# Gate projections moved into seven-product column pairs, with the two plain products of every pair made into filler units of their own

## The chip, the cores and the metric

The kernel runs on one core of one Trainium2 chip. The metric is the device time of one execution in microseconds, as the median of several runs. Engines are named as in the profile: PE is TensorE (matmuls), PEld its weight loads, DVE is VectorE, ACT is ScalarE, POOL is GpSimd, and SP is the engine whose queue issues the DMAs.

## What is computed

A decoder trunk of two layers on 1024 tokens of width 1024. Cut to what matters here:

```python
h = rmsnorm(x, norm1[l])
proj = h @ w_in[l]                        # 1024 x 5120
qa, ka, va, qb, kb, vb, gate_pre = split(proj)
o_a = dilated_mixture(qa, ka, va)         # 12 heads: 4 near, 8 far (two groups)
o_b = stick_breaking_attention(qb, kb, vb)  # 4 heads
g_a, g_b = halves of sigmoid(gate_pre + b_gate[l])
merged = g_a * (o_a @ w_br[l, :256]) + g_b * (o_b @ w_br[l, 256:])
x = x + merged @ w_o[l]
x = x + (gelu(conv(h2 @ w_up gate half)) * (h2 @ w_up value half)) @ w_down[l]
```

The change touches only `h @ w_in[l]`: the columns of the far heads' q, k and v, and the 2048 gate columns.

## The kernel before

**Numbers in two parts.** Every fp32 factor is split into a high and a low part (`split`, L123: ACT copies to the high part, DVE subtracts for the low part). One block product is then three matmuls: high x high, high x low, low x high. A matmul is 128 x 128 weights against 512 tokens.

**Units of projection work.** The normed activations `h` stand in SBUF as `H[n]`, n being the half of the tokens, with eight blocks of 128 features. `gate` (L1077) is a plain unit: it loads 128 gate columns (`weights`, L128), and for each token half runs `product` (L145) over eight blocks, 24 matmuls, copies the result out on ACT and stores it to the DRAM scratch `gs`. `pair` (L943) takes two groups of 128 columns at a time and computes their four results (two column groups, two token halves) with seven block products in place of eight, as Strassen's scheme in Winograd's form does, from sums of weight blocks (formed on POOL and DVE in the unit) and sums of activation blocks (`S[1]` to `S[4]`, formed once per layer in `block_sums`, L888). Each product is `seven` (L879), 12 matmuls. The products go in the order Q1, Q5, Q6, Q3, Q7, Q2, Q4. Two PSUM banks `pa` and `pc` are accumulated further after they have been read: Q1, Q6, Q7 and Q4 go into `pa`, Q5 and Q3 into `pc`, and Q2 has a bank of its own:

```python
yield from seven(pa, w7, S[3], False, True)
dve.tensor_tensor(view(u5), view(u5), grid(pa), ALU.add)
...
pb = bank("ps", "i_b")
yield from seven(pb, w2, half(1, 1), True, True)
...
for word in seven(pa, w4, S[4], False, True):
```

Of the 16 gate column groups per layer, eight are done by `gate` (`PLAIN`, L42) and eight by four `pair_gate` (L1066). Far keys and queries are four `pair_kq` (L1016), far values two `pair_v` (L1039), whose results are also transposed on PE (`v_t`, L1045). So a layer has ten pairs.

**What sets the order.** PE's order is written by the program: `manual_schedule` for PE. ACT, DVE, POOL and SP are ordered by a scheduler. In the attention part of a layer, `attend` (L306) walks the items of attention: stage B (16 stick-breaking items), N (4 near items), T (16 far items). After each of their steps it calls `Dense.advance` (L279) with a rate, and that many steps of filler go in between. One filler step is six matmuls, up to a `yield`. `Dense.choose` (L203) takes first the units in `main` whose conditions hold, then the `plain` ones, then the `seven` ones. A `seven` unit of `main` waits until `plain` is empty. The next unit is made ready while the present one runs: one step for a plain unit, six steps (`READY`, L36), given out at each "turn", for a pair. `RATE` (L41) holds the rates of B, N and the two halves of T. The far items need all far values and the keys of their half, so between N and T some pairs run alone: the pure filler phase. `finish` (L299) drains what is left after the last far item. Then follow the branches with the gates (`br_ps`), `wo_chunk` and the FFN, which the change leaves alone.

**Buffers.** PSUM tags "ps", "s", "t", "o" have two banks each. SBUF tag "pt" (L114) has six buffers of 128 x 512, used by attention and projections, "wr" two for raw weights and for the pair's `u`, "wh" and "wl" four each for split weights, "ql" two for the pairs' raw weights `in_a`.

## Time and profile before

| | |
|---|---|
| median of 3 runs | 2729.11 us (2728.45 to 2729.51) |
| span of the profiled execution | 2728.5 us |
| PE busy | 2677.8 us |
| DVE, ACT, POOL busy | 2016.5, 1353.4, 672.3 us |
| DMA engines busy, over the span | 46.2% |

A row of the stretches view reads: stretch in us, its length, then the busy time of PE, PEld, DVE, ACT and POOL with the number of instructions in brackets, the granted PE clock as a share of full speed, the busy share of the DMA engines, and GB/s. A row of the waits reads: the engine, what waited and its line, behind what; then us in total, how often, and the longest. A row of the timeline reads: start in us, duration, engine, line, operation, and in brackets the idle time before it with what ended it. A row by groups ends with busy us, mean ns of one, and the idle time before. A DMA row ends with the KB of one and the us to its landing. Matmuls are pipelined: a row's duration is longer than the distance to the next start. Attention of layer 0 lies at about 80 to 585 us, that of layer 1 at about 1400 to 1940 us.

### The profile page before, as it was taken

What the parts mean: (1) busy time and instruction counts of PE and PEld (TensorE: products, weight loads), DVE (VectorE), ACT (ScalarE), POOL (GpSimd) and SP (SyncE); (2) the same over time, 40 slices, a digit from 0 to 9 for tenths busy, and PEclk for the clock granted to TensorE, in tenths of its full rate; (3) what the DMA queues carried; (4) which work ended last, traced back from release to release, by engine and by line L of the source; (5) the groups of instructions that cost most, each with busy time, mean ns of one, the idle gap of its engine ahead of it and who ended that gap; (6) DMA issues with size and microseconds to landing.
All of it is one profiled execution on the core that took longest, in us unless ns stands there. A gap on an engine that the chain in (4) does not pass through costs nothing.

```text
span 2728.5 us, 36794 instructions
## 1 busy us (share of the span) xinstructions
PE 2677.8 (98%) x13194; PEld 2245.8 (82%) x13194; DVE 2016.5 (74%) x2976; ACT 1353.4 (50%) x2494; POOL 672.3 (25%) x485
## 2 busy tenths in 40 slices
PE   8999999989999999999999999999999999999999
PEld 8878888878888888888888788888788888888888
DVE  5877656665689888897658776565858888998865
ACT  5655545455455555532346565454635455554225
POOL 1005111112224343421120051211212343443210
PEclk9999999999999999999999999999999999999999
DMA  5012268554334444598410122784732444446863
GB/s 152 21 50 82 63 173 256 183 196 142 93 120 143 155 143 159 188 336 313 175 47 27 52 78 73 198 257 165 250 97 74 147 150 151 170 140 244 331 251 123
DMA packets 356738, 420.52 MB, mean 154 GB/s; under 512 B 20700, under 2 KB 285260, under 8 KB 355020
## 3 DMA queue, kind: packets, MB, share of 16 engines
q1 hardware_dynamic: 356556, 418.18, 46.2%
q8 instruction: 104, 1.70, 0.3%
q14 instruction: 78, 0.64, 0.1%
HBM read 278.59 MB, written 139.53 MB: 153 GB/s over the span
## 4 chain that ended last, share of the span: by engine, by line
PE 66%; DVE 8%; issue 2%; ACT 1%; DMA 1%; POOL 0%; DVEq 0%; ACTq 0%; SPq 0%; POOLq 0%
PE u_a L882 5%; PE u_a L883 5%; PE u_a L884 5%; PE d_ps L1584 4%; PE d_ps L1586 4%; PE d_ps L1585 4%; PE u_c L883 3%; PE u_c L882 3%; PE u_c L884 3%; PE o_ps L150 2%; PE o_ps L151 2%; PE o_ps L152 2%; PE i_a L882 1%; PE u_b L884 1%; PE u_b L882 1%
## 5 line engine op out<-in xcount | busy, mean ns | idle before, releaser
L125 DVE TENSOR_TENSOR w_lo<-up_a,w_hi 128x512 fp32r<-128x512 f32 x240 | 237.4, 996 | 20.5 <-ACT w_hi L124 20.5
L124 ACT CAST w_hi<-up_a 128x512 fp32r<-128x512 f32 x240 | 149.4, 622 | 183.8 <-PE u_a L883 45.4
L1592 DVE TENSOR_TENSOR x<-x,d_ps 128x512 f32<-128x512 f32 (+1 forms) x228 | 151.9, 671 | 77.4 <-PE d_ps L1586 76.1
L1323 POOL TENSOR_TENSOR cv<-cv 128x512 f32<-128x512 f32 x88 | 132.3, 1516 | 249.4 <-DVE cv L1318 139.6
L125 DVE TENSOR_TENSOR w_lo<-w_raw,w_hi 128x512 fp32r<-128x512 f32 x152 | 113.5, 751 | 67.0 <-ACT w_hi L124 63.6
L125 DVE TENSOR_TENSOR g<-cv,g 128x512 fp32r<-128x512 f32 x154 | 152.5, 991 | 5.2 <-ACT g L124 2.7
L124 ACT CAST w_hi<-w_raw 128x512 fp32r<-128x512 f32 x152 | 94.1, 620 | 124.9 <-PE o_ps L151 66.2
L125 DVE TENSOR_TENSOR w_lo<-in_a,w_hi 128x512 fp32r<-128x512 f32 x120 | 87.9, 732 | 82.4 <-ACT w_hi L124 82.1
L124 ACT CAST w_hi<-in_a 128x512 fp32r<-128x512 f32 x120 | 74.5, 621 | 132.3 <-PE i_c L883 52.0
L1584 PE MATMUL d_ps<-gd_in,w_hi 128*128 128x512 f32 (+1 forms) x340 | 130.5, 384 | 1.6 <-issue 0.7
L1586 PE MATMUL d_ps<-gd_in,w_lo 128*128 128x512 f32 (+1 forms) x340 | 129.8, 382 | 0.0
L1585 PE MATMUL d_ps<-gd_in,w_hi 128*128 128x512 f32 (+1 forms) x340 | 129.8, 382 | 0.0
L882 PE MATMUL u_a<-hh,w_hi 128*128 128x512 f32 x320 | 124.6, 390 | 0.7 <-DVE u L1474 0.7
L883 PE MATMUL u_a<-t_lo,w_hi 128*128 128x512 f32 x320 | 124.5, 389 | 0.0
L884 PE MATMUL u_a<-t_hi,w_lo 128*128 128x512 f32 x320 | 124.5, 389 | 0.0
L882 PE MATMUL u_a<-t_hi,w_hi 128*128 128x512 f32 x320 | 124.5, 389 | 0.0
L883 PE MATMUL u_a<-hl,w_hi 128*128 128x512 f32 x320 | 124.5, 389 | 0.0
L884 PE MATMUL u_a<-hh,w_lo 128*128 128x512 f32 x320 | 124.5, 389 | 0.0
L622 DVE TENSOR_TENSOR_SCAN stay<-stay,zero 128x128 f32<-128x128 f32 (+3 forms) x64 | 86.8, 1357 | 38.7 <-ACT stay L620 38.6
L1584 PE MATMUL d_ps<-gd_in,wd 128*128 128x512 f32 (+1 forms) x292 | 113.9, 390 | 0.0
L124 ACT CAST g<-cv 128x512 fp32r<-128x512 f32 x154 | 94.9, 616 | 37.1 <-POOL cv L1323 29.7
L1586 PE MATMUL d_ps<-gd_in,wd 128*128 128x512 f32 (+1 forms) x292 | 112.8, 386 | 0.0
(398 smaller groups left out, 8655.8 us busy)
## 6 DMA issues: line engine op xcount, KB each, us to landing
gd<-g SPq DMA_DIRECT2D x154, 512.0 KB, 3.4
gd_in<-gd SPq DMA_DIRECT2D x154, 512.0 KB, 6.3
up_a<-in_w_up_dram SPq DMA_DIRECT2D x80, 512.0 KB, 5.6
t_kq<-tk SPq DMA_DIRECT2D x32, 768.0 KB, 5.3
wd_raw<-in_w_down_dram SPq DMA_DIRECT2D x22, 1024.0 KB, 8.2
w_raw<-in_w_in_dram SPq DMA_DIRECT2D x80, 256.0 KB, 3.2
in_a<-in_w_in_dram SPq DMA_DIRECT2D x40, 512.0 KB, 4.9
gin<-gs SPq DMA_DIRECT2D x32, 512.0 KB, 4.1
```

What stands on the lines that cost most here:

```text
L124: act.copy(hi, src)
L125: dve.tensor_tensor(lo, src, f32(hi), ALU.subtract)
L150: pe.matmul(o, lh, rh, start=(first and i == 0), stop=False, skip_group_check=share)
L622: dve.tensor_tensor_scan(rev, rev, zero[:, 0:1].to_broadcast([P, L]), 1.0, ALU.mult, ALU.add)
L882: pe.matmul(o, w[0][:, c], rh, start=(first and i == 0), stop=False, skip_group_check=True)
L883: pe.matmul(o, w[0][:, c], rl, start=False, stop=False, skip_group_check=True)
L884: pe.matmul(o, w[1][:, c], rh, start=False, stop=(last and i == 3), skip_group_check=True)
L1323: return lambda: pool.tensor_tensor(dst, a, b, ALU.subtract)
L1584: pe.matmul(o[:, sub], wh[:, c], gh[:, sub], start=(i == 0 and k in (0, 4, 5)), stop=False, skip_group_check=True)
L1585: pe.matmul(o[:, sub], wh[:, c], gl[:, sub], start=False, stop=False, skip_group_check=True)
L1586: pe.matmul(o[:, sub], wl[:, c], gh[:, sub], start=False, stop=(i == m - 1), skip_group_check=True)
L1592: dve.tensor_tensor(x, x, o[:, sub], ALU.add)
```

## The change

All sixteen gate column groups of a layer become eight pairs; `gate` and `PLAIN` go. So a layer has 14 pairs. Each pair is cut in two generators. `ahead` is a plain unit: it computes Q1 = a11 x b11 (12 matmuls), copies it out on ACT and stores it in a DRAM scratch tile of the pair, then adds Q2 = a12 x b21 into the same bank (12 matmuls), which is the finished result for column group 0 and token half 1. `pair_rest` is the remaining seven unit, with five products in the order Q5, Q6, Q3, Q7, Q4; it loads Q1 back from DRAM into `u1` and adds it to the three other results. The plain list holds the `ahead` units of the four key/query pairs, the two value pairs and the eight gate pairs. The sum in place of `H[0]` (`S[4]`) now also waits for the units "01" and "v0". The two rates of stage T go from 0.72 and 0.62 to 0.88 and 0.77. The transposed values go through two small "pt" tiles instead of one of tag "p4".

```diff
-RATE = (0.68, 0.85, 0.72, 0.62)
-PLAIN = 8
+RATE = (0.68, 0.85, 0.88, 0.77)
...
-        series({"plain"}, 4, lambda i: further(4, b21, i), 1, 1)
+        series({"plain", "01", "v0"}, 4, lambda i: further(4, b21, i), 1, 1)
...
+        def ahead():
+
+            w = weights(w_in[l][:, offs[0] : offs[0] + P], P)
+            yield
+            o = bank("ps", "r_ps")
+            yield from product(o, [(w[k], h_part(1, k)) for k in range(4)], share=True)
+            t = small("q1s")
+            act.copy(view(t), grid(o))
+            nc.sync.dma_start(kept_product(key), t)
+            yield
+            yield from product(o, [(w[k], h_part(1, k)) for k in range(4, KD)], first=False, share=True)
+            put(0, 1, grid(o), True)
+            yield
+
+        return ahead, lambda: pair_rest(dense, l, offs, put, view, grid, kept_product(key))
+
+    def pair_rest(dense, l, offs, put, view, grid, kept):
...
         u1, u2 = u[:, HF:T], u[:, 0:HF]
+        nc.sync.dma_start(u1, kept)
...
-        w1 = piece(a11)
-        yield
...
         u5 = small("u5")
         pa, pc = bank("ps", "i_a"), bank("ps", "i_c")
-        yield from seven(pa, w1, half(1, 0), True, True)
-        act.copy(view(u1), grid(pa))
+        yield from seven(pc, w5, S[1], True, True)
+        dve.tensor_tensor(view(u5), view(u1), grid(pc), ALU.add)
         w7 = piece(u2)
-        yield
-        yield from seven(pc, w5, S[1], True, True)
-        act.copy(view(u5), grid(pc))
-        w2 = piece(a12)
-        yield
-        yield from seven(pa, w6, S[2], False, True)
-        act.copy(view(u2), grid(pa))
+        yield "turn"
+        yield
+        yield from seven(pa, w6, S[2], True, True)
+        dve.tensor_tensor(view(u2), view(u1), grid(pa), ALU.add)
...
-        pb = bank("ps", "i_b")
-        yield from seven(pb, w2, half(1, 1), True, True)
-        dve.tensor_tensor(view(u1), view(u1), grid(pb), ALU.add)
-        put(0, 1, u1, False)
-        yield "turn"
-        yield
         for word in seven(pa, w4, S[4], False, True):
             yield "turn"
             yield
-        put(1, 1, grid(pa), True)
+        dve.tensor_tensor(view(u1), view(u1), grid(pa), ALU.add)
+        put(1, 1, u1, False)
...
-            vv = sb.tile([P, 4, 2, P], F32R, tag="p4", bufs=4, name="vv")
+            for r in (0, 2):
...
+                vv = small("vv", F32R).rearrange("p (r h c) -> p r h c", r=2, h=2)
...
-        dense.plain = [gate(l, c) for c in range(PLAIN)]
-        dense.seven = [pair_gate(dense, l, e) for e in range(PLAIN // 2, KD)]
+        vs = {g: pair_v(dense, l, g) for g in (1, 2)}
+        kqs = {(g, pr): pair_kq(dense, l, g, pr) for pr in range(2) for g in (1, 2)}
+        gates = [pair_gate(dense, l, e) for e in range(KD)]
+        dense.plain = [a() for a, _ in [*kqs.values(), *vs.values(), *gates]]
+        dense.seven = [rest() for _, rest in gates]
```

More of the change, by code (lines that the diff above doesn't have):

```diff
@@ L109, in trunk_kernel, with kept_product @@
     dn = [dr.tile([4, T], F32, name=f"dn{i}") for i in range(2)]
+    first_half_product = {}
+    def kept_product(key):
+        if key not in first_half_product:
+            first_half_product[key] = dr.tile([P, HF], F32, name="q1")
+        return first_half_product[key]
     def bank(tag, name):
@@ L943, in pair @@
     def pair(dense, l, offs, tiled, put):
+        key = offs[0]
         def view(x, n=None):
@@ L1045, in turn @@
                 pe.transpose(tp[:, r * P : (r + 1) * P], f[:, r * P : (r + 1) * P], ident)
-            tw = tp.rearrange("p (r h c) -> p r h c", r=4, h=2)
-            vv = sb.tile([P, 4, 2, P], F32R, tag="p4", bufs=4, name="vv")
-            act.copy(vv[:, :, :, 0:64], tw)
-            dve.tensor_tensor(vv[:, :, :, 64:128], tw, f32(vv[:, :, :, 0:64]), ALU.subtract)
-            for h in range(2):
-                there = tv[c][h, :, :, g - 1, n * P : (n + 1) * P]
-                nc.sync.dma_start(there.rearrange("r p c -> p r c"), f32(vv[:, :, h, :]))
+            for r in (0, 2):
+                tw = tp[:, r * P : (r + 2) * P].rearrange("p (r h c) -> p r h c", r=2, h=2)
+                vv = small("vv", F32R).rearrange("p (r h c) -> p r h c", r=2, h=2)
+                act.copy(vv[:, :, :, 0:64], tw)
+                dve.tensor_tensor(vv[:, :, :, 64:128], tw, f32(vv[:, :, :, 0:64]), ALU.subtract)
+                for h in range(2):
+                    there = tv[c][h, r : r + 2, :, g - 1, n * P : (n + 1) * P]
+                    nc.sync.dma_start(there.rearrange("r p c -> p r c"), f32(vv[:, :, h, :]))
             if (c, n) == (1, 1):
@@ L1074, in pair_gate @@
         return pair(dense, l, (OFF_G + e * P, OFF_G + D + e * P), False, put)
-    def gate(l, c):
-        ab, e = c % 2, c // 2
-        cc = ab * KD + e
-        w = weights(w_in[l][:, OFF_G + cc * P : OFF_G + (cc + 1) * P], P)
-        yield
-        for n in range(2):
-            o = bank("ps", "g_ps")
-            yield from product(o, [(w[k], h_part(n, k)) for k in range(KD)])
-            t = small("gt")
-            act.copy(t, o)
-            nc.sync.dma_start(gs[e, n, :, ab, :], t)
-            yield
     def wo_chunk(l, n, e):
@@ L1139, in mixer @@
             *kq("0", 1, {"B17s"}, P, -SCALE),
-            (None, {"N11s"}, pair_v(dense, l, 1), True),
-            *((None, {"N11s"}, pair_kq(dense, l, g, 0), True) for g in (1, 2)),
-            (None, {"N11s"}, pair_v(dense, l, 2), True),
-            *((None, {"N11s"}, pair_kq(dense, l, g, 1), True) for g in (1, 2)),
+            (None, {"N11s"}, vs[1][1](), True),
+            *((None, {"N11s"}, kqs[g, 0][1](), True) for g in (1, 2)),
+            (None, {"N11s"}, vs[2][1](), True),
+            *((None, {"N11s"}, kqs[g, 1][1](), True) for g in (1, 2)),
         ]
```

## The prediction

> **What bounds the kernel now.** I read the page first, then busy time by stretches, then the waits of TensorE, then its timeline around the pairs.

> ```profile
> span 2728.5 us, 36794 instructions
> PE 2677.8 (98%) x13194; PEld 2245.8 (82%) x13194; DVE 2016.5 (74%) x2976; ACT 1353.4 (50%) x2494; POOL 672.3 (25%) x485
> PE 66%; DVE 8%; issue 2%; ACT 1%; DMA 1%; POOL 0%; DVEq 0%; ACTq 0%; SPq 0%; POOLq 0%
> ```
> ```profile
> 900.00:1000.00 100.00, 100.00 (x443) 82.84 (x442) 90.31 (x98) 52.73 (x84) 43.01 (x28) 1.00 0.44 151
> ```
> ```profile
> 340.00:380.00 40.00, 40.00 (x185) 32.86 (x184) 20.05 (x30) 16.84 (x29) 6.00 (x4) 1.00 0.56 153
> ```

> TensorE (PE) is busy 98% of the span and carries two thirds of the chain that ended last. So time follows what PE issues and where PE waits. In the FFN stretch 443 matmuls fill 100 us, 0.226 us each. The stretch 340 to 380 is the pure filler phase of layer 0: pairs alone, because the far items still lack their keys. DVE and ACT are only half busy there, so PE alone sets the pace. Idle PE is 50.7 us in all, and the named waits are mostly in attention:

> ```profile
> PE sb_t L633 <- DVE beta L623: 12.5, 10, 2.4
> PE o L808 <- DVE p1l L125: 5.6, 7, 1.6
> PE o L708 <- DVE p0l L125: 4.5, 2, 2.2
> ```

> **Term 1: fewer matmuls.** A gate column as `gate` costs 2 halves x 8 blocks x 3 = 48 matmuls, a pair of columns 96; with seven products a pair costs 7 x 4 x 3 = 84. Four gate pairs per layer change, so 4 x 12 x 2 layers = 96 matmuls go. The program's instruction counts agree: 13070 on PE before, 12974 after. The other ten pairs per layer keep their 84, now as 24 in `ahead` and 60 in `pair_rest`. What is one matmul worth? Starts of neighbours in the pure phase:

> ```profile
> 345.13 0.39 PE L883 MATMUL i_c<-hl,w_hi 128*128 128x512 f32 x1
> 345.36 0.39 PE L884 MATMUL i_c<-hh,w_lo 128*128 128x512 f32 x1
> 345.58 0.39 PE L882 MATMUL i_a<-t_hi,w_hi 128*128 128x512 f32 x1
> ```

> They start 0.225 us apart, though each is listed as 0.39. In the attention stages the step is about 0.23. So 96 x 0.23 = **-22 us**. [...]

> **Term 2: the sixth product no longer stands between the fifth and the seventh.** Before, `pair` runs Q7 into `pa`, then Q2 into its own bank, then Q4 into `pa`. DVE reads `pa` after Q7 while PE does the 12 matmuls of Q2. The change moves Q2 into `ahead`, so Q4 accumulates into `pa` directly behind Q7, and in the changed program Q4's first matmul waits for DVE's add of `pa` into `u5`. That is a new wait in all 28 pairs. Its length, from rows of the same hand-over:

> ```profile
> 345.85 0.69 DVE L994 TENSOR_TENSOR u<-u,i_c 128x512 f32<-128x512 f32 x1 [1.67 <-PE i_c L884]
> ```
> ```profile
> 595.00 0.68 DVE L1237 TENSOR_TENSOR gin<-gin,br_ps 128x512 f32<-128x512 f32 x1
> ```
> ```profile
> 595.73 0.50 PE L150 MATMUL br_ps<-oh_a,br_w 128*128 128x512 f32 x1 [0.56 <-DVE gin L1237]
> 596.07 0.39 PE L151 MATMUL br_ps<-ol_a,br_w 128*128 128x512 f32 x1
> ```

> An idle DVE starts 0.49 us after the last matmul started (345.36 to 345.85), works 0.69, and PE starts 0.05 after DVE ends (595.68 to 595.73). That is 1.23 instead of 0.23, so 1.00 lost; the first matmul after a wait then takes 0.34 until the next instead of 0.23, so 1.11 in all. What stands between Q7 and Q4 in the changed PE order shortens it: nothing in 16 of the 28 pairs, four small matmuls of a far item in 8 (0.41 us, 1921.58 to 1921.99 below), eight in 2, and eight with the sixteen of `join` in 2.

> ```profile
> 1921.58 0.28 PE L808 MATMUL o<-p1h,t_v 128*128 128x256 f32 x1
> 1921.99 0.44 PE L882 MATMUL i_c<-hh,w_hi 128*128 128x512 f32 x1
> ```

> 16 x 1.11 + 8 x 0.70 + 2 x 0.3 = **+24 us**. Behind the waiting Q4 stand all of PE's later work, the attention items too.

> **Term 3: the read in the middle of `ahead`.** Each of the 28 `ahead` units does 12 matmuls, has ACT copy the bank to `q1s`, then adds 12 more into the same bank. PE waits for that copy. The rows:

> ```profile
> 345.56 0.62 ACT L124 CAST w_hi<-in_a 128x512 fp32r<-128x512 f32 x1 [1.61 <-PE i_c L883]
> ```
> ```profile
> L1086 ACT COPY gt<-g_ps x32: 559/586/589, 144.5 to 1690.3; 128x512 f32<-128x512 f32 x32
> ```

> ACT starts 0.43 after the matmul (345.13 to 345.56) and copies a bank in 0.59. So 0.43 + 0.59 + 0.05 - 0.23 + 0.11 = 0.95, say 0.97. In 9 of the 14 units of a layer the ACT order has a weight split (0.62) right ahead of the copy, released by the last matmul but one; it pushes the copy back by some 0.29, making 1.26. Against that stands the attention work which the PE order has between the halves, from nothing to eight matmuls of scores. Priced by these rows (four score matmuls 0.47, four transposes 0.35), it sums to 6.9 us a layer:

> ```profile
> 300.20 0.28 PE L579 MATMUL z<-kt,qt 128*128 128x256 f32 x1
> 300.67 0.40 PE L150 MATMUL g_ps<-hh,w_hi 128*128 128x512 f32 x1
> ```
> ```profile
> 346.95 0.60 PE L1045 MATMUL v_t<-ident,u 128*128 128x128 f32 x4
> 347.30 0.48 PE L882 MATMUL i_a<-t_hi,w_hi 128*128 128x512 f32 x1
> ```

> (5 x 0.97 + 9 x 1.26 - 6.9) x 2 layers = **+19 us**.

> **What I cost at little or nothing.**

> ```profile
> q1 hardware_dynamic: 356556, 418.18, 46.2%
> ```
> ```profile
> w_raw<-in_w_in_dram SPq DMA_DIRECT2D x80, 256.0 KB, 3.2
> ```
> ```profile
> L125 DVE TENSOR_TENSOR w_lo<-w_raw,w_hi 128x512 fp32r<-128x512 f32 x152 | 113.5, 751 | 67.0 <-ACT w_hi L124 63.6
> ```

> The q1 store and reload (28 each, 256 KB): the reload is issued most of a pair before its use, the store long before that; without that cover each would cost a landing, 3.2 us by the row of that size. The reload waits on SP for a "wr" buffer, and behind it stand the next pair's `in_a` loads and the stores; that buffer's last reader is two pairs back, so I see no delay. `w_raw` gains 24 loads, `in_a` 16: with q1 some 29 MB on 418, and DMA is 46% busy. SP gains 128 issues; in the pure phase a key pair issues 16 stores instead of 20, now in 60 matmuls' time instead of 84. Splits: 24 more `w_hi` and `w_lo` pairs, 0.62 on ACT and 0.75 on DVE, all in stages B and N, where the attention chain itself runs over DVE; evictions that were ACT's become DVE's. The two `v_t` turns per layer that move into B take an "s" bank that scores use. The bound for all this is from below a gain: `RATE` puts more filler under each far item, so the 5.6 us of waits for `p1l` can go, and 72 matmuls instead of 30 are left behind the last `join` to cover the way into the branches, where the waits were

> ```profile
> PE x_t L1110 <- DMA xr<-in_x_dram: 3.2, 1, 3.2
> PE br_ps L150 <- DVE gin L1237: 2.7, 3, 1.7
> ```

> From above it is a longer DVE chain in B: 24 x 0.75 = 18 us of DVE, were it all on the chain. I take 0, nearest to the waits on either side, and keep -12 and +18 for the range.

> **Sum:** -22 + 24 + 19 = +21 on the profiled execution's 2728.5, so **2749 us**. Its span is 0.6 below the median of the three runs (2729.11), which is inside their spread (2728.45 to 2729.51); I add nothing for it.

> **Rivals.**
> *The waits are swallowed (faster).* Place: PE in the attention items. If the chain over DVE and ACT bounds B, N and T, a PE gap ahead of a wait for `beta`, `p0l` or `p1l` costs nothing. Then terms 3 and the far items' part of 2 vanish, the 16 bare gaps stay (17.8), and with the 5.9 us of waits into the branches gone: 2728.5 - 22 + 18 - 6 = 2719. For it: these waits exist. Against: they sum to 22.6 us, in 19 places, and must lie right behind the gaps. It is faster only when more than 26 us are swallowed or saved; between 15 and 26 it is no change.

> *The pair's preparation is late (slower still).* The seven products start with `w5`, which needs `a21 + a22`; `w1`, straight from the load, used to go first.

> ```profile
> in_a<-in_w_in_dram SPq DMA_DIRECT2D x40, 512.0 KB, 4.9
> ```
> ```profile
> L964 POOL TENSOR_TENSOR u<-in_a 128x512 f32<-128x512 f32 x20 | 29.1, 1455 | 119.0 <-DVE w_lo L125 61.7 <-DMA tk<-u 24.3 <-DMA tk<-kq_h 15.7
> ```

> From issue: 4.9 + 2 x 1.46 + 0.7 for `a11` on DVE = 8.5 us, and that DVE step stands ahead of the `u5` add in some pairs, which is due 48 matmuls = 10.9 us after the issue. 2.4 us are spare. Should loads land 4.2 us later with the pairs in quicker succession, 12 pairs lose some 1.8 each: 2749 + 22 = 2771.

> *The clock drops.* Stretches with waits show it:

> ```profile
> 580.00:620.00 40.00, 34.51 (x158) 27.56 (x158) 26.65 (x39) 23.58 (x41) 9.86 (x7) 0.96 0.65 222
> ```
> ```profile
> 1900.00:1940.00 40.00, 38.29 (x217) 32.68 (x216) 28.46 (x55) 25.38 (x51) 4.91 (x5) 1.00 0.63 220
> ```

> With 5.5 us idle the granted clock was 0.96 over 40 us, 1.6 us lost; with 1.7 us idle it stayed at 1.00. If each of the 16 bare gaps cost that: 2749 + 26 = 2775. The second row speaks against it. [...]

> That the change would not remove its 96 matmuls is no rival: the instruction order shows it.

> **Chances.** Forecast, 2735 to 2763: 0.62. Half swallowed, 2724 to 2734: 0.10. Swallowed, about 2719: 0.10. Late preparation, about 2771: 0.12. Clock, about 2775: 0.06. A range of **2724 to 2772** holds the first two and most of the late preparation, and takes in 2749 - 12 and 2749 + 18. A measurement of this kernel tells about 0.2% (5.5 us) from no change: faster 0.10 (the swallowed case), same 0.10 (half swallowed), slower 0.80.

> **What would show it.** The waits of PE should have a new row, `i_a` behind the DVE `u5` add, with 28 or fewer entries of 0.3 to 1.1 us and about 20 us in sum, and a new row `r_ps` behind ACT's `q1s` copy, about 19 us. PE's count falls by 96. The stretches of the pure phase should lose their 40.00 of 40.00. I am wrong if those rows are there but the `sb_t` and `o` rows fall by as much; if `i_c` or `u5` waits for POOL or a DMA show, the preparation is late; if the mean granted clock falls well below this row's, it is the clock.

> ```profile
> core 0: 2728.5 us, clock 0.997
> ```

## The result, and the profile after

The changed kernel takes 2799.82 us (median of 4 runs, 2797.74 to 2806.85) against 2729.19 us for the kernel before on the same chip (4 runs, 2728.45 to 2729.51). The ratio is 1.0261, 95% interval 1.0247 to 1.0276. It is slower, as forecast, but by 71 us where I had said 20. The profiled execution has a span of 2805.0 us, 76.5 more than before.

The page of the kernel after, the lines that answer to those shown of before; below them its mean granted clock, from the view by cores:

```profile
span 2805.0 us, 37073 instructions
PE 2691.6 (96%) x13098; PEld 2244.2 (80%) x13098; DVE 2070.0 (74%) x3104; ACT 1338.3 (48%) x2478; POOL 694.0 (25%) x509
PE 61%; DVE 8%; issue 3%; DMA 3%; ACT 2%; POOL 1%; SPq 0%; DVEq 0%; ACTq 0%; POOLq 0%
```
```profile
core 0: 2805.0 us, clock 0.988
```

PE has 96 matmuls less, and yet 13.8 us more busy time. Part of that comes with the waits: ahead of the gap shown further down (0.98 us, from 360.97 on) the last matmul counts with its listed 0.40 us, where neighbours start 0.23 apart, and the first behind it takes 0.33 until the next starts. So this gap adds some 0.27 us to the busy time. Another part is the clock, whose mean went from 0.997 to 0.988. Idle PE went from 50.7 to 113.4 us. Where it waits, in the waits of PE of the kernel after:

```profile
PE r_ps L155 <- ACT q1s L966: 26.1, 26, 3.0
PE i_a L887 <- DVE u L1019: 22.8, 24, 2.5
PE sb_t L638 <- DVE beta L628: 9.4, 8, 2.2
PE z L584 <- DVE st L795: 8.2, 5, 2.3
PE o L713 <- ACT p0h L129: 6.4, 2, 3.2
...
PE i_c L887 <- DVE u L1003: 3.9, 4, 2.1
PE z L584 <- ACT stay L625: 3.5, 3, 1.2
```

The first two rows are the hand-overs of terms 3 and 2. The other rows are waits of attention and of the pairs. `beta` is lower than it was (12.5), but `z` behind `st` had 1.4 us before and `o` behind `p0h` 0.5, and `i_c` behind a DVE add had no row at all. Busy time by stretches, the one that lost its 40.00 of 40.00, and the FFN stretch, which the change leaves as it was:

```profile
340.00:380.00 40.00, 36.26 (x169) 29.19 (x170) 26.33 (x46) 15.85 (x31) 5.99 (x5) 0.96 0.43 125
900.00:1000.00 100.00, 100.00 (x442) 82.81 (x442) 89.80 (x101) 51.41 (x81) 38.63 (x26) 1.00 0.48 164
```

All of the difference lies in the attention part of the two layers. The next table cuts it into stages by PE's timeline (a stage begins with the first matmul of its kind: `sb_t` for B, the first transpose of N, and so on; the pure filler phase ends with the first `z` from `t_kq`, T with the end of the last matmul of `join`). "Filler" counts the projection matmuls per layer in a stage. "Beyond its work" is the two layers' difference, less the change in filler at 0.23 us each.

| stage | filler before, after | us before (layers 0, 1) | us after | beyond its work |
|---|---|---|---|---|
| B | 558, 558 | 171.0, 170.0 | 178.8, 180.5 | +18 |
| N | 270, 270 | 87.7, 87.6 | 105.6, 105.0 | +35 |
| pure filler | 402, 258 | 95.3, 95.3 | 70.6, 72.3 | +18 |
| T | 420, 474 | 151.4, 149.8 | 177.7, 177.0 | +29 |
| rest, up to the first `br_ps` | 30, 72 | 6.7, 6.7 | 17.7, 17.8 | +3 |
| branches, up to the first `o_ps` | | 59.0, 46.0 | 51.8, 48.7 | -4 |

The sum is +99, and with the -22 of the 96 matmuls +77, the 76.5 of the two spans. B and N hold the same number of filler matmuls as before and are 53 us longer. The forecast had 19 us for them, all of it the waits for `q1s`; these waits lie in B and N and have 26 us of idle time.

How the two hand-overs look, in the timeline of the kernel after. Term 2, PE and then DVE:

```profile
360.57 0.40 PE L889 MATMUL i_a<-t_hi,w_lo 128*128 128x512 f32 x1
361.95 0.50 PE L887 MATMUL i_a<-hh,w_hi 128*128 128x512 f32 x1 [0.98 <-DVE u L1019]
362.28 0.40 PE L888 MATMUL i_a<-hl,w_hi 128*128 128x512 f32 x1
```
```profile
361.21 0.68 DVE L1019 TENSOR_TENSOR u<-u,i_a 128x512 f32<-128x512 f32 x1
```

Term 3, ACT and then PE:

```profile
285.44 0.62 ACT L129 CAST w_hi<-w_raw 128x512 fp32r<-128x512 f32 x1
286.08 0.59 ACT L966 COPY q1s<-r_ps 128x512 f32<-128x512 f32 x1
```
```profile
286.72 0.50 PE L155 MATMUL r_ps<-hh,w_hi 128*128 128x512 f32 x1 [1.10 <-ACT q1s L966]
287.06 0.40 PE L156 MATMUL r_ps<-hl,w_hi 128*128 128x512 f32 x1
287.29 0.56 PE L157 MATMUL r_ps<-hh,w_lo 128*128 128x512 f32 x1
287.65 0.63 PE L155 MATMUL r_ps<-hh,w_hi 128*128 128x512 f32 x1
```

The first, 0.98 us, is the gap that was priced. In the second, ACT does the split right ahead of the copy, as foreseen, and PE waits 1.10 us. But look at the last lines: at about 287.4 the matmuls turn slow. They are listed with 0.63 us instead of 0.40, and their starts lie 0.43 apart (287.65, and the next at 288.08) instead of 0.23. The stretches around that place, cut at 3.41 us:

```profile
284.00:287.41 3.41, 1.69 (x9) 1.08 (x8) 3.40 (x7) 2.57 (x5) 0.00 (x0) 0.99 0.28 77
287.41:290.82 3.41, 3.41 (x11) 2.66 (x10) 3.35 (x6) 0.48 (x1) 0.00 (x0) 0.51 0.44 147
290.82:294.24 3.42, 3.42 (x20) 2.93 (x19) 2.47 (x5) 1.92 (x4) 0.00 (x0) 1.00 0.24 84
```

The granted clock (the third number from the end) is 0.51 in the middle row: 11 matmuls in a full window where the next one has 20. In the row ahead of it PE is busy 1.69 of 3.41 us. That is half a window idle, and no single wait made it: 0.62 us for `p0l` at 285.00 and 1.10 us for `q1s`. So the gap of 1.10 us, with that of 0.62 us near it, cost another 1.7 us (half of the 3.41).

That is a pattern of the whole trace. The half-clock stretches last 3.4 us, in some cases 6.8, and within one run all begin on one grid of 3.41 us (after, the starts of the first and the last, 184.96 and 2024.75, lie 539 steps apart). In the kernel before there are four; the windows ahead of them hold 2.24 to 2.44 us of idle PE, and no other window of its two attention parts has more than 1.72. After, there are 15 (four of them double), behind windows with 1.67 to 3.11 us idle; five other windows with 1.73 to 1.78 were not followed by one. At half a stretch each (0.50 granted), and without the last microseconds of the span, half clock took up to 6.8 us before and up to 32.4 after: 25.6 of the 76.5. These times are upper ends, since PE also waits inside some of the stretches.

Where the 15 lie matters for the account below. The waits in the windows ahead of them are those for `q1s` (six windows, in two of them together with `p0l`, in one with `beta`), `beta`, `p0h`, `p1h`, `st` and `gin`. None lies behind a window in which `i_a` waits, and the two pure filler phases after have no half clock at all.

### The profile page after: what moved, and what is told of

It reads as the page before. It is cut to its first block, busy times and chain, and to the rows that moved or that the text cites. A ratio compares the mean times of both kernels' runs of the same rounds, so it can differ in the third digit from the quotient of the medians.

```text
span 2805.0 us, 37073 instructions
## 1 busy us (share of the span) xinstructions
PE 2691.6 (96%) x13098; PEld 2244.2 (80%) x13098; DVE 2070.0 (74%) x3104; ACT 1338.3 (48%) x2478; POOL 694.0 (25%) x509
## 4 chain that ended last, share of the span: by engine, by line
PE 61%; DVE 8%; issue 3%; DMA 3%; ACT 2%; POOL 1%; SPq 0%; DVEq 0%; ACTq 0%; POOLq 0%
PE u_a L887 5%; PE u_a L888 5%; PE u_a L889 5%; PE d_ps L1590 4%; PE d_ps L1591 4%; PE d_ps L1592 4%; PE u_c L888 3%; PE u_c L889 3%; PE u_c L887 3%; PE o_ps L155 2%; PE o_ps L157 2%; PE o_ps L156 2%; DVE w_lo L130 1%; PE u_b L889 1%; PE u_b L888 1%
## 5 line engine op out<-in xcount | busy, mean ns | idle before, releaser
L130 DVE TENSOR_TENSOR w_lo<-w_raw,w_hi 128x512 fp32r<-128x512 f32 x176 | 127.9, 730 | 80.7 <-ACT w_hi L129 80.2
L129 ACT CAST w_hi<-w_raw 128x512 fp32r<-128x512 f32 x176 | 109.1, 621 | 150.8 <-PE o_ps L156 70.4
L155 PE MATMUL r_ps<-hh,w_hi 128*128 128x512 f32 x224 | 98.6, 440 | 26.1 <-ACT q1s L966 26.1
L988 POOL TENSOR_TENSOR u<-in_a 128x512 f32<-128x512 f32 x28 | 36.8, 1314 | 336.2 <-DVE w_lo L130 89.2
## 6 DMA issues: line engine op xcount, KB each, us to landing
gd<-g SPq DMA_DIRECT2D x154, 512.0 KB, 3.6
gd_in<-gd SPq DMA_DIRECT2D x154, 512.0 KB, 6.7
up_a<-in_w_up_dram SPq DMA_DIRECT2D x80, 512.0 KB, 5.8
in_a<-in_w_in_dram SPq DMA_DIRECT2D x56, 512.0 KB, 5.5
w_raw<-in_w_in_dram SPq DMA_DIRECT2D x104, 256.0 KB, 3.0
gin<-gs SPq DMA_DIRECT2D x32, 512.0 KB, 4.5
```

Of the source, the lines that this page charges most:

```text
L129: act.copy(hi, src)
L130: dve.tensor_tensor(lo, src, f32(hi), ALU.subtract)
L155: pe.matmul(o, lh, rh, start=(first and i == 0), stop=False, skip_group_check=share)
```

## The experiments

Each was timed beside the kernel before on the same chip. That took 2732.18 us (7 runs) beside the first four, 2730.74 (7 runs) beside the second four, and 2731.09 (13 runs) beside the last four. Ratios are to these, with a 95% interval. Where two changed kernels from different sets are compared, the difference is given by the ratios (times 2731 us) and by the times.

Half clock is that of the one profiled execution of each kernel, without its first 30 us and its last microseconds, and it differs between executions of the same kernel. In the four executions of the kernel with both hand-overs mended, for example, the mean granted clock is 0.987 to 0.991, and 0.004 of its span is 11 us. In the ten executions of the kernel with gaps of one read it is 0.995 to 0.998. So differences of a few microseconds of half clock between two of these kernels are not shown to come from the edit.

### The five products in an order that alternates the two banks

The changed kernel with Q6, Q5, Q7, Q3, Q4, which alternate between `pa` and `pc`; the preparation follows that order.

```diff
-        w3 = piece(a11)
+        w7 = piece(u2)
...
+        yield from seven(pa, w6, S[2], True, True)
+        dve.tensor_tensor(view(u2), view(u1), grid(pa), ALU.add)
+        w3 = piece(a11)
...
         yield from seven(pc, w5, S[1], True, True)
         dve.tensor_tensor(view(u5), view(u1), grid(pc), ALU.add)
-        w7 = piece(u2)
...
-        yield from seven(pa, w6, S[2], True, True)
-        dve.tensor_tensor(view(u2), view(u1), grid(pa), ALU.add)
         w4 = piece(a22)
...
+        yield from seven(pa, w7, S[3], False, True)
...
         yield from seven(pc, w3, half(0, 1), False, True)
...
-        yield from seven(pa, w7, S[3], False, True)
```

> Only the order of the five products is changed: Q6, Q5, Q7, Q3, Q4, so that the banks alternate and twelve matmuls stand between a read of a bank and the next product into it. Theory gaps (the waits of PE between two runs of one bank cost their own length, and together with the other waits they pull the granted clock to half for whole stretches): the 22.8 us of waits for the u5 add go, with 3 us of slow restarts, and some 8 of the 18 half-clock stretches of the attention stages (each 1.7 us lost): 2800 - 26 - 13 = 2761, clock about 0.993. Rival load (the clock and the other new waits come from the added splits, stores and fetches): only the waits go, 2774, clock 0.989. Rival feed (the pairs are late in preparation anyway): the waits move to the weights, no more than 8 us gained.

Measured: 2779.29 us (2776.86 to 2781.99), ratio 1.0175 [1.016, 1.019]. The row `i_a` behind the `u5` add (22.8 us) is gone from the waits of PE. In its place `i_a` waits 4.4 us for the weight split of the product that now comes first, and `z` behind `st` has 11.4 us instead of 8.2. Half clock was 25.6 us instead of 32.4, but the mean clocks of the four executions (0.988 to 0.991) are those of the changed kernel (0.988 to 0.990).

What follows: the hand-over of term 2 was worth 20 us by the times and 23 by the ratios, about what its idle time of 22.8 says. Of the forecasts, the one that the waits alone would go (2774) came nearest; that the clock would come back with them (2761) is not borne out.

### Q1 and Q2 of `ahead` in two banks

The changed kernel, with Q2 in a bank of its own and DVE adding the two.

```diff
-            yield from product(o, [(w[k], h_part(1, k)) for k in range(4, KD)], first=False, share=True)
-            put(0, 1, grid(o), True)
+            o2 = bank("ps", "r2_ps")
+            yield from product(o2, [(w[k], h_part(1, k)) for k in range(4, KD)], share=True)
+            t2 = small("q2s")
+            dve.tensor_tensor(view(t2), view(t), grid(o2), ALU.add)
+            put(0, 1, t2, False)
```

> Only the unit ahead is changed: Q2 goes into a bank of its own, and DVE adds it to the copy of Q1, so PE need not wait for the copy. Theory gaps: the 26.1 us of waits for q1s go, with 3 us of restarts, and some 8 half-clock stretches: 2800 - 29 - 13 = 2758, clock about 0.993. Rival load: 2771, clock 0.989; and since the add moves from ACT to DVE in the stages B and N, where the chain runs over DVE, part of that would come back as waits for beta and p0l.

Measured: 2784.54 us (2779.3 to 2788.51), ratio 1.0193 [1.0172, 1.0213]; half clock 23.9 us in the profiled execution, which was the fastest of the four. N went from 105 to 96 us, B stayed at 179. In the waits of PE:

```profile
PE v_t L1063 <- DVE q2s L972: 4.8, 2, 2.4
PE r_ps L155 <- ACT q1s L966: 2.2, 2, 1.1
```

What follows: 24 of 26 us of the `q1s` wait went, and only 15 us of time (19 by the ratios) came back, less than either forecast. Part of the gaps was given back elsewhere: the transposes of the values now wait for the sum `q2s`. The four executions differ with the clock: 2779 and 2781 us at 0.991 and 0.990, 2788 and 2789 us at 0.987 and 0.988.

### Both together

The two diffs above in one kernel.

```diff
+        yield from seven(pc, w5, S[1], True, True)
+        dve.tensor_tensor(view(u5), view(u1), grid(pc), ALU.add)
...
+            o2 = bank("ps", "r2_ps")
```

> Both edits. Theory gaps: both rows of waits go, and the clock returns to about 0.996: 2800 - 55 - 22 = 2723, near the kernel before. Rival load: 2745, clock 0.989, with the new waits of z and o still there. If what the change saves on matmuls (22 us) were to show in full, 2710.

Measured: 2768.45 us (2765.69 to 2770.27), ratio 1.0134 [1.0119, 1.0149]; half clock 23.9 us in the profiled execution. So both hand-overs together are worth 31 us by the times, 35 by the ratios. Half clock is 8.5 us less than in the profiled execution of the changed kernel, but that one was the slowest of its four and this one the fastest of its four; the mean clock of the four executions is 0.9895 there and 0.9890 here. That the clock came back with the two waits is not shown. The kernel is still 36 us above before, with 2.2 us of my two waits left, and both forecasts (2723 and 2745) were far too low. The longest waits of PE now:

```profile
PE z L584 <- DVE st L795: 12.4, 6, 5.5
PE sb_t L638 <- DVE beta L628: 10.6, 10, 2.2
PE o L713 <- ACT p0h L129: 6.4, 2, 3.2
PE o L713 <- DVE p0l L130: 6.3, 8, 1.5
```

The wait for `st` had 8.2 us in the kernel after. In the waits of PE of the kernel before it was

```profile
PE z L579 <- DVE st L790: 1.4, 2, 0.7
```

Its longest case in layer 0 (4.93 us, soon after the start of T; the like place of layer 1 has 5.46) is read from the timelines of DVE and PE in this kernel:

```profile
436.99 0.69 DVE L994 TENSOR_TENSOR in_a<-in_a 128x512 f32<-128x512 f32 x1 [1.18 <-POOL in_a L992]
437.60 0.68 DVE L1030 TENSOR_TENSOR u<-u,i_a 128x512 f32<-128x512 f32 x1
438.19 1.29 DVE L130 TENSOR_TENSOR w_lo<-in_a,w_hi 128x512 fp32r<-128x512 f32 x2
439.40 0.68 DVE L130 TENSOR_TENSOR w_lo<-u,w_hi 128x512 fp32r<-128x512 f32 x1
440.00 1.75 DVE L1043 SCALAR_TENSOR_TENSOR u<-u,kq_h 128x512 fp32r<-128x512 f32 x1
441.67 0.41 DVE L795 CUSTOM_DVE_ANT_1 p<-z,bias 128x256 f32<-128x256 f32 x1
```
```profile
442.15 0.48 PE L584 MATMUL z<-t_kq 128*128 128x128 f32 x1 [4.93 <-DVE st L795]
```

DVE stood waiting 1.18 us, until 436.99, for POOL's sum of the next pair (`in_a`, the step called `a11` in the prediction), and its rows behind that start one after the other up to 441.67: an add of the pair, three splits, another step of the pair's results (L1043), and last the step of attention that PE needs. This is the rival of the late preparation, in a form that the prediction named: the DVE step of `a11` stands ahead of work that is due. In the waits of DVE of the kernel after, with no such row for `in_a` in before:

```profile
DVE in_a L991 <- POOL in_a L989: 37.2, 21, 3.6
```

### The old rates of T

The changed kernel with the old line.

```diff
-RATE = (0.68, 0.85, 0.88, 0.77)
+RATE = (0.68, 0.85, 0.72, 0.62)
```

> The changed kernel with the two rates of stage T put back to 0.72 and 0.62. Theory gaps: the pairs' waits stay the same in number, more of them after the last far item; less filler under each far item brings the waits for p1l back, some 3 us: 2800 to 2806. Rival load (the denser filler in T overloads DVE and the DMA queue there): 2785 to 2795.

Measured: 2797.68 us (2796.57 to 2803.28), ratio 1.0247 [1.0227, 1.0266], against 1.0261 [1.0247, 1.0276] of the change. T shrinks from 178 to 162 us in layer 0 and the rest behind it grows from 18 to 32.

What follows: the rates move filler from one place to another and neither cost nor gain anything that can be measured. The 29 us that T lost are not theirs.

### The sums of weights all on POOL

The kernel with both hand-overs mended, with the sum for `w5` first and the step of DVE moved to POOL, so that DVE's queue no longer waits there.

```diff
-        pool.tensor_tensor(u2, a11, a21, ALU.subtract)
-        pool.tensor_tensor(a21, a21, a22, ALU.add)
+        pool.tensor_tensor(u2, a21, a22, ALU.add)
+        pool.tensor_tensor(a21, a11, a21, ALU.subtract)
         yield
-        dve.tensor_tensor(a11, a21, a11, ALU.subtract)
-        w5 = piece(a21)
+        pool.tensor_tensor(a11, u2, a11, ALU.subtract)
+        w5 = piece(u2)
...
-        w7 = piece(u2)
+        w7 = piece(a21)
```

> The kernel with both edits, and in the pair's preparation the sum a21 + a22, which w5 waits for, is now formed first, and a11 on POOL in place of DVE. Theory late preparation (in the shorter pairs DVE stands in its queue before a11 until POOL and the loads are there, and the far items' reductions and the evictions stand behind it): the waits of DVE for POOL go, the waits of z for the reduction (12.4 us) fall below 6, the stages after N lose some 10 us a layer less: 2768 - 15 = 2753. Rival splits (what is left lies in B and N, from the added splits): 2765 to 2770. Rival DMA (the far items' fetches are late whatever the engines do): z still waits some 10 us, 2765.

Measured: 2755.4 us (2754.3 to 2758.71), ratio 1.0096 [1.0081, 1.0111]; half clock 18.8 us. The row of DVE behind POOL is gone, and PE's wait for `st` fell from 12.4 to 7.8 us (not below 6, as expected).

What follows: the late preparation was real and cost about 0.4%, some 10 us. The profiled execution has 5.1 us less half clock (23.9 to 18.8), but the mean clocks of the four executions overlap (0.987 to 0.991 without the edit, 0.989 to 0.993 with it), so how much of the 10 us came by way of the clock stays open.

### Half of the splits in `ahead`

The kernel with both hand-overs mended, but `ahead` loads and splits only the first four weight blocks and uses them for Q2 as well. The result of column group 0 and token half 1 is then not the reference's; the number of matmuls is the same.

```diff
...
-            w = weights(w_in[l][:, offs[0] : offs[0] + P], P)
+            w = 2 * weights(w_in[l][0:512, offs[0] : offs[0] + P], P, rows=4)
```

> The kernel with both edits, but each unit ahead loads and splits only the first four weight blocks and uses them for Q2 too: Q2 is computed from the wrong weights, and half of the units' splits and loads are left out. Theory splits (two splits of ACT and DVE for every 24 matmuls of filler in place of 48 lengthen B and N, whose PE work is the same as before): B falls from 179 to some 173 us and N from 96 to some 90, both layers: 2768 - 24 = 2744. Rival (the order of the units, v_t and the key stores in B make it): B and N stay within 2 us.

Measured: 2758.2 us (2754.43 to 2760.81), ratio 1.0103 [1.0088, 1.0118] against 1.0134 [1.0119, 1.0149] with all splits: 10 us less by the times, 8 by the ratios, for 28 splits and 28 loads less. N is 4 us shorter in each layer, B is unchanged (178 and 179).

### The kernel before, with more splits

The kernel before, its `gate` unit cut in one unit for each token half. So each half loads and splits its weights again: 16 more loads and splits per layer (32 in all; the change itself has 24 more in all), and twice as many units of half the size.

```diff
-    def gate(l, c):
+    def gate(l, c, n):
...
-        dense.plain = [gate(l, c) for c in range(PLAIN)]
+        dense.plain = [gate(l, c, n) for c in range(PLAIN) for n in range(2)]
```

> The kernel before with each plain gate unit cut in two, one for each token half, each loading and splitting its weights anew: 16 splits and loads more per layer, no new wait of PE on its own banks, nothing else. Theory splits: B and N grow by some 6 us each in each layer, with half-clock stretches: 2729 + 24 = 2753. Rival: the splits find room on ACT and DVE: 2729 to 2733.

Measured: 2744.61 us (2740.46 to 2748.0), ratio 1.0059 [1.0042, 1.0075]. N grew from 87.6 to 93.9 us in both layers, B did not (169.7 and 171.8). In the waits of PE of this kernel there is a row that the kernel after has too:

```profile
PE o L708 <- ACT p0h L124: 6.4, 2, 3.2
```

It is one wait of 3.2 us per layer, in N, and behind it lies a half-clock stretch of 6.8 us. `p0h` is the split of attention weights on ACT, the engine on which the weight splits (0.62 us each) are made. But ACT was not too busy. Its timeline, and DVE's, ahead of the wait at 257 us, and ACT at the same place of the kernel after:

```profile
252.35 0.62 ACT L124 CAST t_hi<-h_sum 128x512 fp32r<-128x512 f32 x1 [5.78 <-POOL h_sum L901]
253.40 0.42 DVE L595 TENSOR_TENSOR ob<-sb_o,fold 64x256 f32<-64x256 f32 x1 [5.26 <-ACT fold L594]
```
```profile
261.56 0.62 ACT L129 CAST t_hi<-h_sum 128x512 fp32r<-128x512 f32 x1 [5.78 <-POOL h_sum L906]
```

ACT stands idle for 5.78 us until POOL has formed a sum of activation blocks (`h_sum`, of `block_sums`), and attention's copy and splits queue up behind it. In the kernel before, no split of `h_sum` waits longer than 1.3 us there. This kernel, the kernel after and all seven made from it have this idle time of 5.77 to 5.79 us on ACT and the 3.2 us on PE, in both layers; the kernel before, the one with a fifth pair and the three with gaps have neither. So by the timelines it is the order of ACT's queue that makes this wait, and not the work of the splits. No run takes it out, and why the scheduler chose that order stays open.

What follows from the last two: splits in N are not hidden, but what is shown of their own cost is the 8 to 10 us of the half of them that was left out. Of the 6.3 us that N grew here in layer 0, 4.7 are waits of PE in N (2.5 us before, 7.2 here, of which 3.2 is the wait for `p0h`) and up to 1.7 the longer half clock behind it.

### The kernel before, with one more pair per layer

The kernel before with six plain gate units instead of eight, and five gate pairs. No `ahead`, no DRAM scratch, no hand-over is added, and 24 matmuls go.

```diff
-PLAIN = 8
+PLAIN = 6
```

> The kernel before with six plain gate columns and five gate pairs in place of eight and four: 24 matmuls fewer in all, no unit ahead, the first pair starts earlier in N. Theory gaps and splits (a gate pair itself costs nothing, what costs is cutting it): 24 x 0.23 = 5.5 us faster, 2723.5, and up to 5 more since more pairs stand behind the last far item. Rival (N without plain filler stalls): 2735.

Measured: 2745.44 us (2741.95 to 2750.25), ratio 1.0059 [1.0043, 1.0074]: 0.6% above before, where I had expected 2723.5. N is 93.6 us with 12 filler matmuls fewer than before. The other stages follow their matmuls (pure filler 75.5 us with 318, rest 27 to 28 us with 120). In its waits of PE:

```profile
PE o L708 <- DVE p0l L125: 10.5, 6, 2.3
PE i_c L884 <- DVE w_lo L125: 5.1, 2, 2.5
```

What follows: the pair in stage N costs more than the plain units whose place it took. The two rows say where: DVE's work for the pair meets that of attention there (`p0l` had 4.5 us before, `w_lo` no row). What is won in matmuls is lost again, so taken in this way the gain of term 1 was not to be had for nothing, even without the new waits.

### Gate units first in the list

The kernel of the sums on POOL, with the `ahead` units of the gates ahead of those of keys, queries and values.

```diff
-        dense.plain = [a() for a, _ in [*kqs.values(), *vs.values(), *gates]]
+        dense.plain = [a() for a, _ in [*gates, *kqs.values(), *vs.values()]]
```

> The kernel with both hand-overs mended and the sums on POOL, with one more edit: the `ahead` units of the gates come first in the plain list, then keys/queries, then values, so that stage B's filler are gate units and the two value units of a layer (transposes into a bank of the scores, more stores) fall into N. It asks what makes B 7 us a layer longer than before (178.3 against 171.0) with the same matmuls. Theory A, the value units do: in B their transposes wait 2.4 us for `q2s`, and `z` waits 1.6 us for a bank that the transposes hold. Then B comes back to 172 to 174 and N takes some of it (97 to 100); total 2748 to 2756. Theory B, every `ahead` unit does (two small results in 24 matmuls instead of one): B stays at 177 or more whatever the order, total 2755 within 3.

Measured: 2755.96 us (2751.59 to 2757.58), ratio 1.0088 [1.0073, 1.0103], as without the edit. B went from 178.3 to 175.1 us in layer 0 and from 176.4 to 174.1 in layer 1, N from 97.0 to 98.2 and 95.4 to 97.9. The waits of PE in stage B of layer 0, without the edit:

```profile
PE sb_t L638 <- DVE beta L628: 5.4, 5, 2.2
PE v_t L1063 <- DVE q2s L972: 2.4, 1, 2.4
PE z L584 <- ACT stay L625: 1.6, 2, 1.2
```

and with it:

```profile
PE sb_t L638 <- DVE beta L628: 8.0, 6, 2.4
```

What follows: neither theory fully. The value units did make the waits of `v_t` and `z` in B, which are gone there, and 2 to 3 us of B with them; but `beta` waits longer, and 4 us per layer of B's growth are left whatever the order. Splits did not lengthen B in the two experiments above, so what remains is the other work of an `ahead` unit; no run takes it apart. The time moved into N (over the span `v_t` now waits 7.5 us instead of 4.8), so nothing was won.

### Gaps of three sizes in the pure filler phase of the kernel before

Three kernels test the clock by itself, in the phase that had no idle PE. In the kernel before, Q2 and Q4 of the key, query and value pairs change places, so that Q4 follows Q7 in the same bank behind one DVE read; in the second and third kernel, DVE reads the bank twice and three times. The diff is that of the third, cut; the second has the subtraction alone, so one of its results lacks a product.

```diff
         dve.tensor_tensor(view(u5), view(u5), grid(pa), ALU.add)
+        for op in (ALU.subtract, ALU.add) if tiled else ():
+            dve.tensor_tensor(view(u5), view(u5), grid(pa), op)
         put(1, 0, u5, False)
...
+        if not tiled:
             pb = bank("ps", "i_b")
             yield from seven(pb, w2, half(1, 1), True, True)
...
         for word in seven(pa, w4, S[4], False, True):
...
+        if tiled:
+            pb = bank("ps", "i_b")
+            yield from seven(pb, w2, half(1, 1), True, True)
```

> Before, with Q2 and Q4 of the key, query and value pairs in the other order (Q7, Q4, Q2), so that Q4 follows Q7 in one bank and TensorE waits there for DVE's one read. 12 gaps, most in the pure filler phase, which was without any idle time and at full clock. It is the first of a series of three with gaps of about 1.1, 1.8 and 2.5 us. Theory A (the clock halves in the 3.4 us after a 3.4-us window with 1.7 us of idle TensorE or more): a gap of 1.1 us never does it alone; no half clock in the pure phase, 12 x 1.1 = 13 us, total 2742. Theory B (half clock comes with attention, not with the idle time): the same here, 2742.

> As the one before, but DVE reads the bank twice (u5 gets the product added and taken off again, so that product is missing in the result): gaps of 1.11 + 0.69 = 1.8 us, just at the bound. Theory A: a gap that falls into one window as a whole (about half of them) is followed by half clock: 12 x 1.8 = 22 and some 5 x 1.7 = 8, total 2759, with half-clock stretches of 3.4 us in the pure phase. Theory B: 2751, the pure phase at full clock throughout.

> As the one before, but with three reads (added, taken off, added: the result is the full one): gaps of 2.5 us. Theory A: some two thirds of the gaps have 1.7 us or more in one window: 12 x 2.5 = 30 and 8 x 1.7 = 14, total 2773, with half-clock stretches behind most of the gaps in the pure phase and none behind those cut evenly by a window's edge. Theory B: 2759, the pure phase at full clock throughout.

Measured: 2737.98 us (2735.8 to 2741.38), ratio 1.0025 [1.0015, 1.0034]; 2757.67 (2756.65 to 2758.95), 1.0097 [1.0082, 1.0112]; 2771.83 (2770.71 to 2775.15), 1.0152 [1.0136, 1.0169]. From the waits of PE of the three, in that order:

```profile
PE i_a L882 <- DVE u L999: 7.0, 10, 0.8
```
```profile
PE i_a L882 <- DVE u L1001: 19.0, 10, 2.0
```
```profile
PE i_a L882 <- DVE u L1001: 29.0, 12, 2.7
```

The stretch 340 to 380 of the same three, which was 40.00 of 40.00 at 1.00 before:

```profile
340.00:380.00 40.00, 38.44 (x176) 31.12 (x175) 20.01 (x29) 15.74 (x27) 5.18 (x4) 1.00 0.52 143
```
```profile
340.00:380.00 40.00, 36.04 (x152) 28.85 (x151) 17.93 (x26) 13.42 (x24) 3.89 (x3) 0.91 0.47 131
```
```profile
340.00:380.00 40.00, 34.60 (x147) 27.83 (x145) 19.28 (x28) 13.37 (x23) 3.87 (x3) 0.91 0.43 122
```

The gaps came out at 0.78, 1.98 and 2.70 us instead of the 1.1, 1.8 and 2.5 foreseen, so the total times alone do not decide between the theories; the clock in the pure phase does. With gaps of 0.78 us the clock stays at 1.00 and the phase is 4.1 us longer for its four gaps. With 1.98 and 2.70 us it falls to 0.91 over 40 us: two half-clock stretches of 3.4 us each. The eight gaps of 1.98 us in the pure phases of the second kernel show on what it depends here. Its grid follows from its nine half-clock stretches, whose starts agree within 0.1 us; cut by that grid, the gaps fall so:

| gap begins at | part in the first window, part in the next | half clock behind it |
|---|---|---|
| 349.14 | 1.98, 0 | yes, from 351.9 |
| 373.51 | 1.98, 0 | yes, from 375.8 |
| 396.43 | 1.98, 0 | yes, from 399.7 |
| 419.85 | 0.32, 1.66 | no |
| 1720.30 | 0.33, 1.65 | no |
| 1743.06 | 1.47, 0.51 | no |
| 1764.37 | 0.64, 1.34 | no |
| 1786.16 | 1.98, 0 | yes, from 1788.9 |

The same gap of 1.98 us, at the same hand-over of the same program, is followed by half clock or is not, by whether it falls into one window: all four that lie whole in one window are, and the four that are cut, with at most 1.66 us in one, are not. In the third kernel seven of the eight gaps of 2.70 us are followed by half clock; the eighth was cut into 1.90 and 0.80. The first of them in the stretches cut by the grid:

```profile
348.50:351.91 3.41, 1.43 (x6) 0.86 (x5) 2.47 (x4) 0.62 (x1) 0.00 (x0) 1.00 0.83 230
351.91:355.33 3.42, 3.42 (x11) 2.73 (x10) 0.41 (x1) 0.59 (x1) 0.00 (x0) 0.50 0.00 0
355.33:358.74 3.41, 3.41 (x18) 2.83 (x17) 1.06 (x3) 1.69 (x3) 1.26 (x1) 1.00 0.50 154
```

There is no attention work in that phase. So half clock follows the idle time of PE there (0.50 behind 1.98 us in one window), and theory B of the three is out. The sizes fit too: layer 0 of the second kernel has 13.7 us more in its pure phase, four gaps at 2.2 us (8.8) and three half-clock windows at 1.7 (5.1); layer 1 has 10.4 more, four gaps (8.8) and one window (1.7).

## Why the prediction was wrong in size

**Right: the sign, terms 1 and 2, and the mechanism of term 3.** The 96 matmuls went. The wait of `i_a` has 22.8 us in 24 places (I had said 24 us and about 20 in the row). That of `r_ps` has 26.1 us, where I had said 19: four of its waits are 1.9 to 3.0 us long, since there the copy stands behind more work on ACT than the one weight split I had counted. Taken out, the two give 31 to 35 us and not the 49 of their rows, since other waits come in their place: a part is swallowed, as the first rival said, but it is not what decides.

**Wrong: the step "What I cost at little or nothing".** I took 0 and kept +18 as its upper end. With both hand-overs mended the kernel is 36 us above before, and 22 us of matmuls are gone: so what I had put at 0 costs 58 us, half clock included. B and N are there still some 17 us a layer longer than before with the same matmuls. What the runs show of it:

- *The splits.* I had put 24 more `w_hi` and `w_lo` pairs at nothing. Leaving out 28 of them gave 8 to 10 us.
- *The order of ACT's queue.* I looked at what ACT has to do and not at what it stands waiting for. The wait of PE for `p0h` in N rose from 0.5 to 6.4 us because ACT waits 5.78 us for POOL ahead of it, and the half-clock stretch at that place is double in both layers where it was single before. No run takes this out.
- *The order of evictions and preparation on DVE.* It was a rival at 0.12, with a price of +22 us; it came true beside the forecast, not instead of it. It was worth some 10 us where it was taken out.
- *The units of keys and values moved into B.* I named the "s" bank that the transposes take and put it in the same 0; those waits exist (2.4 and 1.6 us in layer 0, with both hand-overs mended and the sums on POOL), and removing them only moves the time.

**Wrong: the clock, at 0.06.** I weighed a single gap of 1.1 us against the row of 1900 to 1940, which has 1.7 us idle over 40 us and a clock of 1.00. For a gap by itself that holds: with gaps of 0.78 listed us the clock stayed at 1.00. But the change puts its gaps among those of attention, and what counted is the sum within 3.41 us (0.62 and 1.10 us in the window ahead of 287.4). A stretch of 40 us has nearly twelve such windows, and the row could say nothing on how its 1.7 us were spread (1.55 of them lay in one window). I had the evidence in the other row: 5.5 us idle and 0.96, one half-clock stretch, was a window with 2.3 us of them. That the price agrees (26 us said on top of the forecast, 25.6 in the profiled execution) is luck: I had priced the 16 bare gaps of term 2, and not one of the 15 half-clock stretches lies behind a gap of that kind. They lie behind the `q1s` waits and behind waits of attention.

In these runs about half a window of idle PE was enough: 1.98 us in one window, all four times in the pure phases of the second kernel with gaps, and also in parts, as the 0.62 and 1.10 us show.

**What stays open.** With both hand-overs mended and the sums on POOL, the kernel is 25 us above before, so 47 above what the matmuls alone would make it. In the profiled execution up to 12 of these are half clock (18.8 against 6.8); the splits are some 8 to 10 by the run that left half of them out, and the wait for `p0h` is 6 more than before. By stages of that execution, beyond their work, it is 14 in B, 17 in N, 12 in T, 8 in the pure phase and -5 on the way into the branches, half clock included. The 20 or so that are left were not taken apart further, and the parts named may overlap. No version here beats the kernel before.

## What to carry to other kernels

Filler work is not priced by its matmuls alone. In a stage where attention runs over ACT and DVE, look at the splits and evictions that a filler unit brings, and above all at where the scheduler puts them: here ACT, busy 48% of the span, stood idle for 5.78 us for a late input, with attention's copy and splits behind it, and PE waited 3.2 us for one of them. When a change adds short waits, do not price them one by one: cut the trace by the grid on which its half-clock stretches begin (3.41 us here) and add up what is idle in each piece: gaps of 0.78 us alone left the clock at 1.00, and one of 1.10 us with one of 0.62 in the same piece was followed by 0.51. And before a product is moved away from between two others, look whether it was the cover of a read: an order that alternates banks, as in the first experiment, took that wait of 22.8 us out again and kept the matmuls saved.
